# Neighbourhood attention in a two-layer encoder: scores as plain fp32 matmuls on 64x32 pieces with five key blocks per 32 queries, the product with v on 64x64 quarters

## The chip, the cores and the metric

One core of a Trainium2 chip runs the whole program. The metric is the device time of one execution in microseconds, the median over several runs. Engines are named as in the profile: PE is TensorE, DVE VectorE, ACT ScalarE, POOL GpSimd, SP the SyncE queue that issues nearly all DMAs.

## What is computed

Two encoder layers over 512 tokens with 1024 features and 16 heads of 64. Layer A mixes tokens with dilated sliding-window attention in three groups, layer B with attention over a two-dimensional neighbourhood. The change is in layer B alone. Its tokens form a grid of 8 rows and 64 columns; queries are taken in blocks of 16 columns, and each block sees a slab of 32 columns in all 8 rows, masked to the 16 columns round the query, with a learned bias by row and column distance:

```python
def mixer_b(hn, w_in, w_out, q_gain, k_gain, rpb):
    q, k, v, gate = jnp.split(hn @ w_in, 4, axis=-1)
    q = rms_norm(q.reshape(b, s, N_HEADS, HEAD_DIM), q_gain) * (HEAD_DIM ** -0.5)
    k = rms_norm(k.reshape(b, s, N_HEADS, HEAD_DIM), k_gain)
    ...
        logits = jnp.einsum('bhcqd,bhrcjd->bhcqrj', qr, kr) + bias
        logits = jnp.where(col_valid[:, :, None, :], logits, NEG_INF)
        p = jax.nn.softmax(logits.reshape(b, N_HEADS, n_cb, NA_COL_BLOCK, wr * NA_SLAB), axis=-1)
        out = jnp.einsum('bhcqrj,bhrcjd->bhcqd', p, vr)
    ...
    y = y * jax.nn.silu(gate)
    return y @ w_out
```

Every layer is `x + mixer(rms_norm(x))`, all in float32. The kernel returns the final x, transposed by the host's layout.

## The kernel before

**Precision.** The large projections are done in fp32r. A value is split into a high part (a cast) and a low part (value less high), and `mm3` adds three products: high by high, high by low, low by high. ScalarE casts the high part of each weight (`wh`, L133), VectorE or GpSimd subtracts for the low part (`wl`, L139). Activations are split in the same way (`hn_h`, `hn_l`, and `y` in two halves). Layer A's attention uses plain fp32 matmuls on pieces of the array: scores on 64x32, the product with v on 64x64 quarters (`by_quarters`), whose two halves of the keys lie in two PSUM banks. `whole` puts these together: ScalarE copies the one (L803), VectorE adds the other (L804).

**Order.** TensorE's order is written by the program. A generator `main` yields after each piece of projection (`acc`), a generator `side` holds the attention; `run` interleaves them by a simulated clock that each matmul advances. For layer B the table `B_PLAN` says at which clock the scores and the values of each of eight head pairs (0 to 7) come. Values of a pair wait, besides, for its weights to be back from DRAM. `later_on` puts off a DMA or a small job by simulated time, `chores` are the halves of the gate's function (`silu`, L817). The other engines run in order too; a scheduler merges their instructions, and `keep_in_program_order` holds some in the order in which they are written. SP issues in order. PSUM has eight banks: four for `acc`, four (`bank`) for all the rest.

**Layer B's attention** for one head pair:

- the projection leaves q and k, ScalarE evacuates them (`rawq`, L544), GpSimd squares (L312), VectorE sums (L313); the inverse root comes from small steps on VectorE or GpSimd (L113 to L125); VectorE multiplies (L332, four instructions) and transposes (L737, two), and DMAs bring q and k into the layout of the scores (`bd`, then `vv` or `rawq`).
- `side_b` splits q and k into `qkb`: ScalarE L1226, L1227 and L780, VectorE L1228 and L1232, GpSimd L1229 for a copy of q's edge.
- scores: 24 fp32r matmuls on 64x128 pieces, 256 columns each, into four banks `log`.
- softmax: VectorE adds the bias `eb` and takes the minimum (the sign is turned), ScalarE exponentiates (L1276) and scales (L1282); rows are 256 wide, or 128 with two parts.
- the weights are transposed in 32x32 pieces (L905), written to DRAM and read back (`pt`, L918) so that keys lie on partitions.
- values: `side_by_side`, 12 matmuls (24 records) on 128x64 pieces into one bank `o`.
- `put_y`: VectorE multiplies with the gate (L858), ScalarE casts the high part of y (L861), GpSimd subtracts for the low part (L864); for pair 7 VectorE does.

**The out product** (`out_product`) multiplies y with the output weights into eight tiles of 128 features: four in `acc` banks over the first six pairs, then three in `acc2` banks over the same, then pairs 6 and 7 (`late`) for all seven, then the eighth tile in two halves of the tokens. Between pairs' values stand the `acc` matmuls of this product. `residual` loads the x to be added into the memory that held `pt`; it is written to SP's queue after values 6 and after values 7.

Of the kernel before, what the change touches and what calls it, by code (L numbers as in the profile page):

```python
# [22 lines left out]
P = 128  # L23
# [9 lines left out]
LINE = 384 + 2 * 448  # L33

# [12 lines left out]
    ("scores", 7, 176700), ("values", 5, 180000), ("values", 6, 198000), ("values", 7, 213000),  # L47
# [5 lines left out]
def tile_hybrid_encoder(  # L53
# [41 lines left out]
    eb_d = dr.tile([16, P, 384], F32, name="eb_d")  # L95
# [46 lines left out]
    def blocks():  # L142

        for hc in range(NHC):
            b = hc * A_HC
            first = hc == NHC - 1
            yield from ((b + 512 * KT * (i ^ first), 512, KT) for i in range(2))
            if hc == NHC - 1:
                yield b - A_HC + 1152 * KT, 128, KT
            yield b + 1024 * KT, 128, KT  # L150
            if hc != NHC - 2:
                yield b + 1152 * KT, 128, KT
        yield from outs(A_OUT, 1)
# [5 lines left out]
        yield from outs(B_OUT, 2)  # L159

    def outs(b, late):

        k = KT - late
        for n, ks in ((512, k), (384, k)) + ((512, 1), (384, 1)) * late + ((128, KT),):
            yield b, n, ks
            b += n * ks
# [12 lines left out]
    def splits():  # L179
# [22 lines left out]
        while ahead:  # L202
            raw, cols, n = ahead.pop(0)
            step = 384 if n == 384 else 512
            for c in range(0, cols, step):
                queue.append((*split(raw[:, c : c + step], step), min(n, step)))
# [30 lines left out]

    def mm3_heads(os, lh, ll, rh, rl, last):

        for n, (l, r) in enumerate(((lh, rh), (lh, rl), (ll, rh))):  # L240
            for hd in range(2):
                hs = slice(64 * hd, 64 * hd + 64)
                matmul(os[hd], l(hs), r(hs), share=2, start=(n == 0), stop=(last and n == 2))
# [220 lines left out]
    def bias_rows():  # L464
# [10 lines left out]
        def spread_out(rows, cols, first, n, src, o):  # L475
            dst = bass.AP(
                eb_d.tensor, eb_d.offset + rows * 16 * 384 + first * 384 + cols, [[16 * 384, 32], [384, n], [1, src[1]]]
            )
            t, width = src[0], src[0].shape[1]
            tc.keep_in_program_order(  # L480
                nc.sync.dma_start(
                    dst, bass.AP(t.tensor, t.offset + rows * width + o, [[width, 32], [-8, n], [1, src[1]]])
                )
            )

        for n, r in enumerate(range(0, P, 32)):
            later_on(30000 + 40000 * n, partial(spread_out, r, 0, 0, 16, (lb_d, 256), 120))
            later_on(45000 + 40000 * n, partial(spread_out, r, 256, 0, 8, (gb_d, P), 56))
            later_on(55000 + 40000 * n, partial(spread_out, r, 256, 8, 8, (gb_d, P), 120))
# [292 lines left out]
    def side_by_side(o, mms, first=True):  # L782


        for i, (d, v, r) in enumerate(mms):
            for hd in range(2):
                hs = slice(64 * hd, 64 * hd + 64)
                matmul(d(o[hs]), v(hs), r(hd), start=(first and i == 0), stop=(i == len(mms) - 1))

# [95 lines left out]
    def bias_b(hc):  # L885
        e = wk.tile([P, 2, 384], F32, tag="e12", name="eb")
        for hd in range(2):
            m = nc.sync.dma_start(e[:, hd, :], eb_d[2 * hc + hd].rearrange("(r c) x -> c r x", r=8))
            tc.keep_in_program_order(m)
        return e  # L890
# [229 lines left out]
    def out_product(key, sink, late, halves=False):  # L1120
# [5 lines left out]
        def step(k, tiles, hl=None):  # L1126
            h, l = hl or next(wsteps)
            for f in tiles:
                i = f if f < 4 else (f - 4) % 3
# [20 lines left out]
        for f in range(4, 7):  # L1150
            acc[f] = bank("acc2")
        for k in range(KT - late):
            yield from step(k, range(4, 7))
        for k in range(KT - late, KT):
            yield key, k, "y"
            yield from step(k, range(4))
            yield from step(k, range(4, 7))
        acc[7] = ps_acc.tile([P, 512], F32, tag="acc", name="acc")
        if not halves:
            for k in range(KT):  # L1160
                yield from step(k, (7,))
# [49 lines left out]

    def side_b(hc):
        if hc >= 1 and hc + 1 < NHC:
            st["e", hc + 1] = bias_b(hc + 1)
        raw = st.pop(("raw", hc))
        e = st.pop(("e", hc))
        landed, left = raw
        assert not left[0]
        qk = wk.tile([P, 2 * EXT + 2 * S], F32R, tag="q12", name="qkb", bufs=1)
        qh, ql = qk[:, :EXT], qk[:, EXT : 2 * EXT]  # L1220
        kh, kl = (qk[:, 2 * EXT + S * n : 2 * EXT + S * n + S].rearrange("p (t x) -> p t x", t=4) for n in range(2))
        tokens = lambda t: t[:, :S].rearrange("p (i t r) -> p t i r", i=4, t=4)
        src = lambda f: landed[:, :, f, :]
        q_src = src(0).rearrange("p t (i r) -> p t i r", i=4)
        first = lambda t: t[:, S:EXT].rearrange("p (t r) -> p t r", t=2)
# [6 lines left out]
        m = nc.vector.scalar_tensor_tensor(kl, src(1), gk[:, 3:4], kh.bitcast(F32), op0=ALU.mult, op1=ALU.subtract)  # L1232
        tc.keep_in_program_order(m)
        yield 3800
        pt, turners = pq[:, 2048 * (hc % 2) : 2048 * (hc % 2) + 2048], []

        at = lambda a, hd, i: 448 * a + 224 * hd + 32 * i

        def scores(u):
            lgs = lgs_of[u] = [bank("log") for _ in range(2)]  # L1240
            for b in (2 * u, 2 * u + 1):
                i0, step = (b, 1) if b < 3 else (0, 3)
                m = lambda t_, hs: sb(t_[hs], 32 * i0, [[32 * step, 2], [P, 4], [1, 32]])
                qs = slice(64 + P * b, 192 + P * b)
                o = 256 * (b % 2)
                mm3_heads(
                    [lg[:, o : o + 256] for lg in lgs],
                    lambda hs: qh[hs, qs], lambda hs: ql[hs, qs], lambda hs: m(kh, hs), lambda hs: m(kl, hs), True,
                )

        lgs_of = {}

        def softmax(hd, u, lg):
            pr = wk.tile([P, 512], F32, tag="p", name="p", bufs=4)
            mns = wk.tile([P, 8], F32, tag="mnb", name="mns", bufs=4)
            for b in (2 * u, 2 * u + 1):
                mn = mns[:, 4 * (b % 2) : 4 * (b % 2) + 4]
                o = 256 * (b % 2)
                if b < 3:
                    parts = ((slice(0, P), o),)  # L1260
                    n, ec = 256, 0
                else:
                    parts = ((slice(0, 64), o + P), (slice(64, P), o))
                    n, ec = 128, 256
                for rows, c in parts:
                    nc.vector.tensor_tensor_reduce(
                        out=pr[rows, o : o + n],
                        in0=lg[rows, c : c + n],
# [246 lines left out]
```

## Time and profile before

| | |
|---|---|
| median of 3 runs | 806.82 us (806.59 to 807.04) |
| profiled execution | 806.53 us, its span 804.7 us |
| PE busy | 799.6 us (99%) |
| DVE, ACT, POOL busy | 538.9 (67%), 447.8 (56%), 230.1 us (29%) |
| waits of PE that the profile lists | 0.9, 0.6, 0.4, 0.2 us |
| layer B's scores and values in the chain | 8 times about 1.64, 8 times about 1.69 us |

A line of the profile is read so: the chain gives start, duration, engine, the program's name and line, and the number of records. In groups, `64*32 64x128` is the piece of the array and the shape (partitions x columns), then the count, the busy time, the mean of one in ns, and the idle time of the engine just before. In the timeline `x4` groups neighbours, and the bracket gives the idle time before and what ended it. A plain fp32 matmul has two records, an fp32r matmul one.

### The profile page before, as it was taken

The page shows a single profiled execution, that of the slowest core. Times are in us where ns is not written, and L with a number is a line of the kernel's source. Part 1 is how long each engine was busy: PE and PEld are TensorE (multiplying, and loading weights), DVE is VectorE, ACT ScalarE, POOL GpSimd, SP SyncE. Part 2 cuts the span into 40 slices and gives each one's busy share as a digit, 9 for nine tenths or more (in the row PEclk, how much of TensorE's full clock was granted, in tenths as well). Part 3 has the DMA queues.
Part 4 walks back from the last instruction along what each step waited for, and adds up shares of the span by engine and source line. Part 5 has one row for each costly group of instructions (what it writes and reads, how often), then busy time and mean ns, then how long its engine had stood idle before and what let it go on. Part 6 is the DMA issues. An engine that isn't in the chain of part 4 may idle for free.

```text
span 804.7 us, 16419 instructions
## 1 busy us (share of the span) xinstructions
PE 799.6 (99%) x6078; PEld 655.5 (81%) x6078; DVE 538.9 (67%) x1375; ACT 447.8 (56%) x934; POOL 230.1 (29%) x372
## 2 busy tenths in 40 slices
PE   9999999999999999999999999999999999999998
PEld 7888888888888888888888888888888887778787
DVE  7474575676577577477567766638646989997824
ACT  7442745745745744754654675436346675757721
POOL 3242432442441532532432331110312224040100
PEclk9999999999999999999999999999999999999999
DMA  8578587877977976977987955167264797698664
GB/s 291 159 204 255 164 223 236 241 212 204 267 215 221 306 226 208 305 221 209 273 239 217 279 177 168 44 226 241 84 201 124 223 258 204 201 269 238 179 210 158
DMA packets 93585, 172.58 MB, mean 214 GB/s; under 512 B 12160, under 2 KB 51216, under 8 KB 93504
## 3 DMA queue, kind: packets, MB, share of 16 engines
q1 hardware_dynamic: 93360, 171.26, 72.1%
q8 instruction: 48, 0.79, 0.4%
q14 instruction: 33, 0.27, 0.1%
q10 hardware_dynamic: 144, 0.26, 0.1%
HBM read 127.84 MB, written 49.82 MB: 221 GB/s over the span
## 4 chain that ended last, share of the span: by engine, by line
PE 93%; DVE 3%; ACT 3%; DMA 1%; POOL 0%; issue 0%; SPq 0%; DVEq 0%
PE acc L227 83%; PE log L227 5%; PE o L227 4%; ACT p L1276 1%; PE tp L231 1%; DVE wl L139 1%; ACT p L1282 1%; DMA wraw<-in_w 1%; DVE rawq L332 0%; ACT rawq L544 0%; ACT wh L133 0%; DVE rawq L737 0%; PE pa L227 0%; POOL sq L312 0%; ACT x L426 0%
## 5 line engine op out<-in xcount | busy, mean ns | idle before, releaser
L227 PE MATMUL acc<-wh,hn_h 128*128 128x512 f32 x704 | 277.3, 395 | 0.4 <-ACT rawq L544 0.4
L227 PE MATMUL acc<-wl,hn_h 128*128 128x512 f32 x704 | 273.7, 390 | 0.6 <-POOL wl L139 0.6
L227 PE MATMUL acc<-wh,hn_l 128*128 128x512 f32 x704 | 273.6, 389 | 0.0
L133 ACT CAST wh<-wraw 128x512 fp32r<-128x512 f32 (+1 forms) x259 | 157.7, 612 | 207.1 <-PE acc L227 180.0
L139 DVE TENSOR_TENSOR wl<-wraw,wh 128x512 fp32r<-128x512 f32 (+1 forms) x188 | 137.5, 734 | 145.5 <-ACT wh L133 145.0
L139 POOL TENSOR_TENSOR wl<-wraw,wh 128x512 fp32r<-128x512 f32 (+1 forms) x72 | 96.7, 1342 | 231.2 <-ACT wh L133 197.0
L227 PEld LDWEIGHTS acc<-wh,hn_h 128*128 128x128 f32 x704 | 132.1, 188 | 31.8 <-issue 3.3
L227 PEld LDWEIGHTS acc<-wh,hn_l 128*128 128x128 f32 x704 | 132.1, 188 | 27.9
L227 PEld LDWEIGHTS acc<-wl,hn_h 128*128 128x128 f32 x704 | 132.2, 188 | 27.7 <-POOL wl L139 1.4
L312 POOL TENSOR_TENSOR sq<-rawq 128x256 f32<-128x256 f32 (+1 forms) x82 | 59.9, 741 | 108.4 <-ACT rawq L544 95.5
L227 PE MATMUL acc<-y,wh 128*128 128x512 f32 (+1 forms) x272 | 81.5, 383 | 0.0
L997 ACT ACTIVATE p<-p,mn 128x512 f32<-128x512 f32 (+1 forms) x64 | 44.8, 701 | 60.3 <-DVE mn L986 60.3
L227 PE MATMUL acc<-hn_h,wh 128*128 128x512 f32 x192 | 75.7, 394 | 0.0
L227 PE MATMUL acc<-hn_l,wh 128*128 128x512 f32 x192 | 74.8, 389 | 0.0
L227 PE MATMUL acc<-hn_h,wl 128*128 128x512 f32 x192 | 74.7, 389 | 0.0
L905 DVE STREAM_TRANSPOSE tr<-p 128x512 f32<-128x512 f32 (+1 forms) x88 | 59.0, 681 | 20.8 <-ACT p L824 11.4
L313 DVE TENSOR_REDUCE ss<-sq 128x4 f32<-128x256 f32 (+1 forms) x96 | 47.6, 506 | 31.9 <-POOL sq L312 31.4
L227 PEld LDWEIGHTS acc<-y,wh 128*128 128x128 f32 x272 | 48.8, 188 | 9.4 <-issue 0.9
L227 PE MATMUL acc<-y,wl 128*128 128x512 f32 (+1 forms) x136 | 51.3, 377 | 0.0
L332 DVE TENSOR_TENSOR rawq<-rawq,rs 128x256 f32<-128x256 f32 (+1 forms) x96 | 48.2, 563 | 2.3 <-POOL rs L125 1.9
L544 ACT ACTIVATE rawq<-acc,rs_n 128x512 f32<-128x512 f32 (+1 forms) x76 | 45.8, 613 | 0.3
L824 ACT ACTIVATE p<-p,mn 128x512 f32<-128x512 f32 (+1 forms) x64 | 44.3, 700 | 2.1 <-DVE mn L823 2.0
(144 smaller groups left out, 918.7 us busy)
## 6 DMA issues: line engine op xcount, KB each, us to landing
wraw<-in_w SPq DMA_DIRECT2D x119, 512.0 KB, 5.6
td<-tr SPq DMA_DIRECT2D x14, 1024.0 KB, 8.1
pt<-td SPq DMA_DIRECT2D x56, 256.0 KB, 4.6
qd<-rawq SPq DMA_DIRECT2D x7, 1536.0 KB, 7.2
qt<-qd SPq DMA_DIRECT2D x28, 384.0 KB, 6.6
td<-tr SPq DMA_DIRECT2D x8, 896.0 KB, 5.4
pt<-td SPq DMA_DIRECT2D x32, 224.0 KB, 6.7
bd<-rawq SPq DMA_DIRECT2D x8, 512.0 KB, 3.2
```

The lines of the kernel that those rows point to most:

```text
L133: nc.scalar.copy(h, raw)
L139: eng.tensor_sub(l, raw, h.bitcast(F32))
L227: nc.tensor.matmul(o, l, r, **kw)
L231: nc.tensor.transpose(o, i, ident)
L312: nc.gpsimd.tensor_mul(to, v, v)
L313: nc.vector.tensor_reduce(ss[:, i * ns : (i + 1) * ns], sq.rearrange("p (a b) -> p a b", b=64), axis=AX.X, op=ALU.add)
L332: m = nc.vector.tensor_mul(v, v, by)
L544: nc.scalar.activation(dst, src, AF.Copy, scale=rs_n[:, i : i + 1])
L824: nc.scalar.activation(pr, pr, AF.Copy, scale=mn[:, 3:4])
L905: nc.vector.transpose(dst, src[:, :n].rearrange(order, b=4, k=32, **({"g": 2} if apart else {})))
L997: nc.scalar.activation(row, row, AF.Exp, bias=mn[:, 1:2], scale=-1.0, accum_out=mn[:, 2:3])
L1276: nc.scalar.activation(pr[:, o : o + n], pr[:, o : o + n], AF.Exp, bias=mn[:, 0:1], scale=-1.0, accum_out=mn[:, 2:3])
```

## The change

Layer B's q and k are no longer split. The scores take q as it landed and one tile `kx` in which ScalarE puts k, scaled; GpSimd copies 64 columns at each end, so that any five neighbouring blocks of 32 keys are contiguous. For each of 16 blocks of 32 queries and both heads there is one fp32 matmul of 160 columns on a 64x32 piece. Softmax rows are all 160 wide, and the bias in DRAM is laid out for that (14 writes instead of 12, eight loads per pair instead of two, into a tile kept for two pairs). Twelve small transposes take the place of four. The weights go through DRAM in half key tiles, each with 192 queries (six blocks, `RUN`).

The values use `by_quarters` and `whole` from layer A: 32 fp32 matmuls into two banks, ScalarE's copy and VectorE's add after them. As two banks are now used, the out product of layer B holds two tiles in `acc2` (`more` = 2) rather than three; the seventh tile is its own pass over the eight pairs, after the late ones. The weights are laid out in that order. In `B_PLAN` the values of pair 7 are due at 207000 instead of 213000.

```diff
-    ("scores", 7, 176700), ("values", 5, 180000), ("values", 6, 198000), ("values", 7, 213000),
+    ("scores", 7, 176700), ("values", 5, 180000), ("values", 6, 198000), ("values", 7, 207000),
...
     def side_b(hc):
-        tc.keep_in_program_order(nc.scalar.copy(tokens(qh), q_src))
-        tc.keep_in_program_order(nc.scalar.copy(first(qh), landed[:, 0:2, 0, 0:32]))
-        tc.keep_in_program_order(nc.vector.tensor_sub(tokens(ql), q_src, tokens(qh.bitcast(F32))))
-        nc.gpsimd.tensor_copy(ql[:, S:EXT], ql.bitcast(F32)[:, 0:64])
-        yield 700
-        tc.keep_in_program_order(scaled(kh, src(1), 3))
-        m = nc.vector.scalar_tensor_tensor(kl, src(1), gk[:, 3:4], kh.bitcast(F32), op0=ALU.mult, op1=ALU.subtract)
-        tc.keep_in_program_order(m)
-        yield 3800
+        kx = wk.tile([P, 20 * 32], F32, tag="e12", name="kx")
+        mid = kx[:, 64 : 64 + S].rearrange("p (i t r) -> p t i r", i=4, t=4)
+        tc.keep_in_program_order(scaled(mid, landed[:, :, 1, :].rearrange("p t (i r) -> p t i r", i=4), 3))
+        nc.gpsimd.tensor_copy(sb(kx, 0, [[576, 2], [1, 64]]), sb(kx, 128, [[320, 2], [1, 64]]))
+        yield 3500
...
         def scores(u):
+            lgs = [bank("log") for _ in range(2)]
+            for t in (2 * u, 2 * u + 1):
+                o = W5 * (t % 2)
+                for j in range(4):
+                    k = 32 * (4 * j + t)
+                    for hd in range(2):
+                        hs = slice(64 * hd, 64 * hd + 64)
+                        matmul(lgs[hd][32 * j : 32 * j + 32, o : o + W5], landed[hs, t, 0, 32 * j : 32 * j + 32],
+                               kx[hs, k : k + W5], share=2, start=(t % 2 == 0), stop=(t % 2 == 1))
...
         def weigh():
-            o = bank("o")
-            side_by_side(o, mms)
-            return o
+            os = [bank("o") for _ in range(2)]
+            jobs = [(n, m, RUN * m + 128 * n, 4, P * m) for m in range(4) for n in range(2)]
+            for m in range(3):
+                jobs += [(0, m + 1, RUN * m + 256, 2, P * m + 64), (1, m, RUN * m + RUN, 2, P * m + P)]
+            jobs += [(0, 3, 3 * RUN + 320, 1, 480), (1, 0, 0, 1, 0)]
...
+            by_quarters(os, mms)
+            return whole(os)
...
-    def out_product(key, sink, late, halves=False):
+    def out_product(key, sink, late, more):
-        for f in range(4, 7):
+        for f in range(4, 4 + more):
             acc[f] = bank("acc2")
...
+        for f in range(4 + more, KT):
+            acc[f] = ps_acc.tile([P, 512], F32, tag="acc", name="acc")
+            if f == 7 and more < 3:
+                break
             for k in range(KT):
-                yield from step(k, (7,))
+                yield from step(k, (f,))
```

The order of the instructions moves with it. In the changed kernel lines have other numbers: L332 is L329, L737 is L733, L804 is L792, L817 is L805, L858 is L846, L861 is L849, L864 is L852, L139 is L142, L227 is L231, L1208 is L1206, L780 is L776.

The first place is round the scores of pair 3. VectorE in the kernel before, from the low parts of q and k (`qkb`) to the transposes of the next head norm; `gt` is the gate of pair 1, which is multiplied with `o`, `na` and `rs` are steps of the head norm's inverse root, `rawq` is what it scales:

```order
L1228 TENSOR_TENSOR qkb<-vv,qkb 128x4x4x32
L120 SCALAR_TENSOR_TENSOR na<-na,nv 128x16
L1232 SCALAR_TENSOR_TENSOR qkb<-vv,gk,qkb 128x512
L858 TENSOR_TENSOR gt<-gt,o 128x512
L1208 TENSOR_TENSOR gx<-acc,rs_half 128x512
L121 SCALAR_TENSOR_TENSOR rs<-na,rs 128x16
L332 TENSOR_TENSOR rawq<-rawq,rs 128x2x4x32 x4
L139 TENSOR_TENSOR wl<-wraw,wh 128x512
L737 STREAM_TRANSPOSE rawq<-rawq 128x2x256 x2
```

VectorE at the same place after the change:

```order
L123 SCALAR_TENSOR_TENSOR na<-na,nv 128x16
L1206 TENSOR_TENSOR gx<-acc,rs_half 128x512
L124 SCALAR_TENSOR_TENSOR rs<-na,rs 128x16
L142 TENSOR_TENSOR wl<-wraw,wh 128x512
L121 TENSOR_TENSOR na<-rs 128x16
L123 SCALAR_TENSOR_TENSOR na<-na,nv 128x16
L124 SCALAR_TENSOR_TENSOR rs<-na,rs 128x16
L329 TENSOR_TENSOR rawq<-rawq,rs 128x2x4x32 x4
L733 STREAM_TRANSPOSE rawq<-rawq 128x2x256 x2
L792 TENSOR_TENSOR ow<-ow,o 128x512
L846 TENSOR_TENSOR gt<-gt,ow 128x512
```

The multiplication of pair 1 stood ahead of the head norm's products; now it stands, with the add of the two halves (`ow`), behind products and transposes. GpSimd, same place, before: the copy of q's edge (`qkb`) for pair 3, the last steps of an inverse root, then the low part of pair 1's y.

```order
L1229 CAST qkb<-qkb 128x64
L113 TENSOR_SCALAR nv<-ss 128x16
L114 TENSOR_SCALAR rs<-nv 128x16
L118 TENSOR_TENSOR na<-rs 128x16
L123 TENSOR_TENSOR na<-na,nv 128x16
L124 TENSOR_SCALAR na<-na 128x16
L125 TENSOR_TENSOR rs<-rs,na 128x16
L118 TENSOR_TENSOR na<-rs 128x16
L864 TENSOR_TENSOR y<-gt,y 128x512
```

And after:

```order
L126 TENSOR_TENSOR na<-na,nv 128x16
L127 TENSOR_SCALAR na<-na 128x16
L128 TENSOR_TENSOR rs<-rs,na 128x16
L852 TENSOR_TENSOR y<-gt,y 128x512
L1247 COPY kx<-kx 128x2x64
```

The copy for pair 3 stood ahead of the low part of y and now stands behind it. On ScalarE the key's copy for pair 3 (L776) likewise follows the cast of pair 1's y (L849).

The second place is the end of the out product. TensorE before, round the values of pair 7 (`o`); the first four `acc` rows and the three `acc2` tiles (`acc_8927` to `acc_8929`) still belong to pair 6, and the last row reads the y of pair 7:

```order
L227 MATMUL o<-pt,rawk 64x128 x2
L227 MATMUL acc<-y,wh 128x512 x2
L227 MATMUL acc<-y,wl 128x512
L227 MATMUL acc<-y,wh 128x512 x2
L227 MATMUL acc<-y,wl 128x512
L227 MATMUL acc_8927<-y,wh 128x512 x2
L227 MATMUL acc_8927<-y,wl 128x512
L227 MATMUL acc_8928<-y,wh 128x512 x2
L227 MATMUL acc_8928<-y,wl 128x512
L227 MATMUL acc_8929<-y,wh 128x512 x2
L227 MATMUL acc_8929<-y,wl 128x512
L227 MATMUL acc<-y,wh 128x512 x2
```

TensorE there after the change; `acc_9211` and `acc_9212` are the two `acc2` tiles for pair 6, and the last row reads the y of pair 7:

```order
L231 MATMUL o<-pt,rawk 64x128 x16
L231 MATMUL o<-pt,rawk 64x64 x12
L231 MATMUL o<-pt,rawk 64x32 x4
L231 MATMUL acc_9211<-y,wh 128x512 x2
L231 MATMUL acc_9211<-y,wl 128x512
L231 MATMUL acc_9212<-y,wh 128x512 x2
L231 MATMUL acc_9212<-y,wl 128x512
L231 MATMUL acc<-y,wh 128x512 x2
```

Fifteen matmuls stood between values 7 and its first reader, six do now. VectorE there after the change, with the two halves of the gate's function (L805) between the add and the multiplication:

```order
L792 TENSOR_TENSOR ow<-ow,o 128x512
L805 SCALAR_TENSOR_TENSOR gt<-eg,gt 128x256 x2
L846 TENSOR_TENSOR gt<-gt,ow 128x512
L142 TENSOR_TENSOR wl<-wraw,wh 128x512
L852 TENSOR_TENSOR y<-gt,y 128x512
```

Before, L817 and L858 followed each other with no add ahead of them, and nothing stood between L858 and L864.

More of the change, by code (lines that the diff above doesn't have):

```diff
@@ L158, in blocks, with outs @@
             b += n * KT
[L159 to L164, printed above, removed]
+        yield from outs(B_OUT, 2, 2)
+    def outs(b, late, more):
+        k, m = KT - late, P * more
+        for n, ks in ((512, k), (m, k)) + ((512, 1), (m, 1)) * late + ((128, KT),) * (4 - more):
             yield b, n, ks
@@ L1308, in side_b @@
+            by_quarters(os, mms)
+            return whole(os)
+        lgs_of = [scores(u) for u in range(2)]
         held = []
-        for u in range(2):
-            scores(u)
         for u in range(2):
```

222 lines of the change are left out of this document (106 added, 116 removed).

## Prediction

> **What bounds the kernel now.** I read the page first, then the waits, the chain, and the timeline round the places that the change touches.
>
> ```profile
> span 804.7 us, 16419 instructions
> PE 799.6 (99%) x6078; PEld 655.5 (81%) x6078; DVE 538.9 (67%) x1375; ACT 447.8 (56%) x934; POOL 230.1 (29%) x372
> PE 93%; DVE 3%; ACT 3%; DMA 1%; POOL 0%; issue 0%; SPq 0%; DVEq 0%
> ```
>
> TensorE is the bound: 99% busy and 93% of the chain. The waits say how little it stands still.
>
> ```profile
> PE busy L398 <- DVE warm L387: 0.9, 1, 0.9
> PE acc L227 <- POOL wl L139: 0.6, 1, 0.6
> PE acc L227 <- ACT rawq L544: 0.4, 1, 0.4
> PE log L227 <- DVE qkb L1232: 0.2, 1, 0.2
> ```
>
> So a shorter attention block is won in full, and a new wait of TensorE is lost in full, unless an engine that feeds it comes late. The profiled execution took 806.53 us, 1.83 more than its span; the median of the three runs is 806.82. I sum against 806.53 and add 0.29. A measurement can tell about 0.2% from no change: faster is under 805.2, slower over 808.4.
>
> **The blocks on TensorE.** The chain has scores and values of layer B (24 instructions) and, already in the form to which they go, layer A's (96 and 120). An fp32 matmul shows as two records, an fp32r one as one.
>
> ```profile
> 510.15 1.84 PE log L227 x96
> 523.35 2.72 PE o L227 x120
> 608.41 1.64 PE log L227 x24
> 610.05 22.64 PE acc L227 x99
> 769.63 1.69 PE o L227 x24
> L227 PE MATMUL log<-qt,q 64*32 64x128 f32 x896 | 19.5, 271 | 0.0
> L227 PE MATMUL log<-k,q 64*32 64x256 f32 x224 | 9.5, 382 | 0.0
> L227 PE MATMUL o<-pt,v0x 64*64 64x128 f32 x256 | 10.3, 270 | 0.0
> L227 PE MATMUL o<-pt,v0x 64*64 64x64 f32 x192 | 7.1, 217 | 0.0
> ```
>
> The 64x32 pieces grow from 271 to 382 ns over 128 columns, 0.87 ns a column. Eight run side by side. Layer A's block is 64 records of 128 columns, 16 of 192 and 16 of 256, 160 on average, so 96 x 160/8 = 1920 columns deep: 1.67 us and a remainder of 0.17. The new scores are 64 records of 160 (4 query tiles x 4 blocks x 2 heads x 2 records), 1280 deep: 1.11 + 0.17 = 1.28; by records alone, 1.84 x 64/96 = 1.23. I take 1.30 against 1.64: 0.34 less, bounds 0.24 and 0.41.
>
> The 64x64 quarters grow by 53 ns over 64 columns, 0.83 ns a column, four side by side. Layer A's 2.72 us hold 64 records of 128 columns and 56 of 64, 11776/4 = 2944 deep, so 2.44 + 0.28. The new values have per head 8 jobs of 128 columns, 6 of 64 and 2 of 32, 1472 in all; two heads and two records over four quarters leave 1472 deep: 1.22 + 0.28 = 1.50; by records 2.72 x 64/120 = 1.45. I take 1.48 against 1.69: 0.21 less, bounds 0.14 and 0.33. Eight of each: -4.4 us (bounds -3.0 and -5.9).
>
> One rule speaks against this. The Trainium skill, "TensorEngine Tiling (Array Packing)", section Instruction Overhead, gives each matmul about 60 cycles whatever its columns, and warns against tiling a dimension that is already small. As an estimate at that page's 60 cycles and the 2.4 GHz of "TensorE: Matmul & The Clock Gate", 64 records would take 1.6 us, the blocks would save under 1 us in all, and the sum would be near 811. Layer A's row disagrees, 96 records in 1.84 us being 19 ns each, and the row decides.
>
> **The splits go.** Scores 4 waited in its middle for the key's low part:
>
> ```profile
> 693.48 0.39 PE L227 MATMUL log<-qkb 64*128 64x256 f32 x2
> 694.04 1.59 PE L227 MATMUL log<-qkb 64*128 64x256 f32 x22 [0.18 <-DVE qkb L1232]
> ```
>
> The third matmul starts 0.56 after the first; at 1.59/22 = 0.07 each it would have been 0.14. The wait goes: -0.4 us (bounds -0.2, the wait as the profile books it, and -0.4). The splits' other instructions on VectorE, ScalarE and GpSimd lie beside TensorE's work and count nothing. The 0.4 for ScalarE's `rawq` I leave standing; at most it goes too.
>
> **A new wait at scores 3.** Here the order moves. The product of head pair 1 now ends in a copy and an add (`ow`), and VectorE has that add and the following multiplication behind four products and two transposes of the key's head norm. ScalarE's key copy for pair 3 stands behind the cast of y, and GpSimd's copy of the key's edge behind its subtraction. TensorE's scores 3 wait for both copies. All that follows on TensorE waits with them. Before, the multiplication stood ahead of the products:
>
> ```profile
> 669.11 0.41 DVE L313 TENSOR_REDUCE ss<-sq 128x4 f32<-128x256 f32 x1
> 669.44 0.17 DVE L120 SCALAR_TENSOR_TENSOR na<-na,nv 128x16 f32<-128x16 f32 x1
> 669.73 0.69 DVE L139 TENSOR_TENSOR wl<-wraw,wh 128x512 fp32r<-128x512 f32 x1
> 671.88 0.69 DVE L858 TENSOR_TENSOR gt<-gt,o 128x512 f32<-128x512 f32 x1
> 672.49 0.68 DVE L1208 TENSOR_TENSOR gx<-acc,rs_half 128x512 f32<-128x512 f32 x1
> 672.60 0.62 ACT L861 CAST y<-gt 128x512 fp32r<-128x512 f32 x1 [2.03 <-DVE gt L858]
> 673.29 2.58 DVE L332 TENSOR_TENSOR rawq<-rawq,rs 128x256 f32<-128x256 f32 x4
> 674.11 1.47 POOL L864 TENSOR_TENSOR y<-gt,y 128x512 fp32r<-128x512 f32 x1
> 676.41 1.29 DVE L737 STREAM_TRANSPOSE rawq<-rawq 128x512 f32<-128x512 f32 x2
> 676.82 1.70 PE L227 MATMUL log<-qkb 64*128 64x256 f32 x24
> 642.49 1.39 DVE L332 TENSOR_TENSOR rawq<-rawq,rs 128x256 f32<-128x256 f32 x4
> L804 DVE TENSOR_TENSOR ow<-ow,o 128x512 f32<-128x512 f32 x8 | 5.5, 687 | 11.5 <-ACT ow L803 11.5
> L471 POOL COPY lb<-rp 128x128 f32<-128x128 f32 x1 | 0.3, 291 | 0.1
> ```
>
> On this clock the last reduction ends at 669.52. Five small steps at 0.17, one `gx` at 0.68 and one `wl` at 0.69 bring VectorE to 671.74. The four products take 1.39 where GpSimd is idle and 2.58 where it subtracts y; now that subtraction comes later and only GpSimd's small norm steps run, so I take 2.0, nearer the first: 673.74. Transposes 1.29, add 0.69, multiplication 0.69: 676.41. Cast 0.62, subtraction 1.47: 678.5. The edge copy (128x128 in a row of 0.29): 678.8. ScalarE's key copy, of the cast's size and right behind it, is done by then. TensorE comes at 676.82 less three `acc` matmuls that now follow the scores (22.64/99 = 0.23 each) less 0.21 of the shorter values: 675.93. A wait of 2.9 us. With 1.39 and y in 1.30 (another row of it, below) it is 2.1; with 2.58 it is 3.4.
>
> On the 2.0 the Trainium skill, "SBUF — State Buffer", section Who interferes with whom, says that a VectorE instruction with two SBUF inputs contends with a GpSimd one that reads SBUF. By it the products would go at 1.39 wherever GpSimd rests, and the wait would be 2.3; the two rows agree, but GpSimd doesn't rest here throughout.
>
> **A new wait at y of pair 7.** Between values 7 and the first matmul that reads its y there were 15 `acc` matmuls; now 6.
>
> ```profile
> 785.29 0.75 DVE L817 SCALAR_TENSOR_TENSOR gt<-eg,gt 128x256 f32<-128x256 f32 x2
> 787.55 0.69 DVE L858 TENSOR_TENSOR gt<-gt,o 128x512 f32<-128x512 f32 x1 [1.50 <-PE o L227]
> 788.92 0.69 DVE L864 TENSOR_TENSOR y<-gt,y 128x512 fp32r<-128x512 f32 x1 [0.69 <-ACT y L861]
> L803 ACT COPY ow<-o 128x512 f32<-128x512 f32 x8 | 4.7, 587 | 24.9 <-PE o L227 24.9
> ```
>
> Before, y was there 2.06 us after values 7 ended (787.55 to 789.61), under 15 x 0.23 = 3.4 us of cover. Now: copy 0.59, add 0.69, the two gate steps (0.75, which ran before the block ended and now stand behind the add), multiplication 0.69, cast 0.62, subtraction 0.69: 4.03, and some 0.1 for a `wl` between. The cover is 6 x 0.23 = 1.4, and the first of the reading matmuls needs only the cast: 1.6. 4.1 to 4.2 less 1.6: +2.6 us (2.2 to 3.0), with nothing behind it to take it up.
>
> **The rest of the tail.** Values 7 comes 48 `acc` matmuls (10.9 us) after values 6, instead of 63 (14.5). Its input is read behind the residual's loads:
>
> ```profile
> 771.36 1.56 SPq L1175 DMA_DIRECT2D pt<-xm_d  x2
> 773.13 1.30 POOL L864 TENSOR_TENSOR y<-gt,y 128x512 fp32r<-128x512 f32 x1 [9.16 <-ACT y L861]
> 773.44 1.85 SPq L918 DMA_DIRECT2D pt<-td  x4
> DMA to landing us min/median/max: 5.5/6.1/6.8
> ```
>
> The fourth read issues at about 774.9 and lands by 781.7 at most, 10.4 after values 6 ended at 771.3. It just fits; I take +0.3 with the y of pair 5 (0 to 1.3). Eight bias loads for two on SyncE's queue, each about 0.4 to issue: some 2.5 us more delay per pair, against reads that, in the pair just shown, lie 4 us ahead of their block. Nothing.
>
> Sum: -4.4 - 0.4 + 2.9 + 2.6 + 0.3 = +1.0. On 806.53 that is 807.5, on the median 807.8.
>
> **Rivals.** (a) One of the two waits is absent: the order says who stands behind whom, and VectorE could come to pair 1's add sooner than row times say. For it: VectorE loses two splits per pair. Against: its norm chain starts from sums that GpSimd and TensorE release. Without scores 3's wait, 804.9; without y's, 805.2; without both, 802.3. Chance 0.17, mostly faster.
>
> (b) Pair 7's reads come late. The place is values 7, the point a landing of over 10.9 us after values 6, half a microsecond past the row above; every microsecond over is paid. For it: residual loads of the same queue land together with them. Against: the row, 6.8 at most. At a landing of 8.3 instead of 6.8 it costs 1.0 beside my 0.3, at 9.3 it costs 2.0: 808.8 to 809.8. Chance 0.20, mostly slower.
>
> (c) The wait at scores 3 lets TensorE's rate fall. After its first idle stretch TensorE ran ten matmuls at 0.45 each, twice the 0.23 later:
>
> ```profile
> 0.92 4.46 PE L398 MATMUL busy<-ones 128*128 128x512 f32 x10 [0.92 <-DVE warm L387]
> ```
>
> If that came back for as long, 4.46 us at half rate lose 2.2: 810.0. It decides from a wait that no row has, since the longest is 0.9. "TensorE: Matmul & The Clock Gate", Trainium skill, in its section on M=128, puts it at a whole window of about 3.4 us idle; my 2.9 stays below, my upper bound reaches it. Chance 0.07, slower.
>
> **The numbers.** My own case has 0.56: 0.38 within 0.2%, 0.15 slower, 0.03 faster; by the bounds of its terms, not all at once, 805.9 to 809.6. With (a) faster 0.14 and same 0.03, (b) same 0.05 and slower 0.15, (c) slower 0.07: faster 0.17, same 0.46, slower 0.37. The range takes in one absent wait below and (b) and (c) above.
>
> **What would show it.** Right: score blocks near 1.30 and value blocks near 1.48 in the chain; among TensorE's waits one of about 3 us before scores 3, put down to GpSimd's `kx`, and one of about 2.6 after values 7, put down to `y`. Wrong: blocks no shorter than 1.64 and 1.69, either wait below 1 us, or a wait over 1 us at another place.

## The result and the profile after

The changed kernel takes 812.54 us in the median (810.42 to 816.14, seven runs), the kernel before 806.82 (806.58 to 807.27, seven runs): a ratio of 1.0071, interval 1.0052 to 1.0090. The forecast was 807.8, and its dearest rival, (c), 810.0; the direction was left open, and the measured time lies beyond both. The spread is new: the kernel before stays within 0.7 us, the changed one within 5.7. Part of it shows in the mean granted clock of TensorE, where 1.000 is full speed: 1.000 in the run of 810.42, 0.998 in 811.09 and 812.93, 0.996 in the other four, which still lie 4.3 us apart. The profiled execution is the slowest of the seven, 816.14, with a span of 814.3, so its waits are not those of a usual one. One execution of e7 (891.66 us) and one of e10 (2054.52 us) below stand far outside of the others, and the times given leave them out.

First the page of the changed kernel, then TensorE's waits in it.

```profile
span 814.3 us, 17799 instructions
...
PE 799.7 (98%) x6718; PEld 655.7 (81%) x6718; DVE 527.0 (65%) x1398; ACT 441.3 (54%) x925; POOL 228.8 (28%) x373
```

```profile
PE log L231 <- POOL kx L1247: 5.0, 2, 2.6
PE acc L231 <- ACT y L849: 1.8, 1, 1.8
PE o L231 <- DMA pt<-tdb: 1.5, 1, 1.5
PE acc L231 <- ACT rawk L540: 1.5, 1, 1.5
```

Five places, where one or two were forecast: `kx` twice (scores 3 and scores 7), the y of pair 7, the weights of pair 7, and an evacuation. Set side by side by the count of `acc` matmuls, the two executions differ as follows. A wait is counted here from start to start, which makes it up to 0.5 us longer than the idle time in the list of waits:

| place | us against before |
|---|---|
| eight scores, eight values on TensorE | -4.3 |
| old stalls at scores 4 and ahead of the evacuation near 703 | -1.0 |
| scores 3: wait 2.5, then slow matmuls | +4.1 |
| evacuation near 730 | +1.7 |
| scores 7: wait 2.7, then slow matmuls | +4.1 |
| values 7 (wait 1.6) and y of pair 7 (2.5) | +4.3 |
| before layer B | +0.5 |
| sum (measured at the last matmul: +9.5) | +9.4 |

**Scores 3**, the timeline of the changed kernel, VectorE, ScalarE, GpSimd and TensorE:

```profile
668.47 0.41 DVE L310 TENSOR_REDUCE ss<-sq 128x4 f32<-128x256 f32 x1
...
670.79 1.47 DVE L329 TENSOR_TENSOR rawq<-rawq,rs 128x256 f32<-128x256 f32 x4
672.30 1.30 DVE L733 STREAM_TRANSPOSE rawq<-rawq 128x512 f32<-128x512 f32 x2
...
673.53 0.65 DVE L792 TENSOR_TENSOR ow<-ow,o 128x512 f32<-128x512 f32 x1
...
674.21 0.75 DVE L846 TENSOR_TENSOR gt<-gt,ow 128x512 f32<-128x512 f32 x1
675.00 0.62 ACT L849 CAST y<-gt 128x512 fp32r<-128x512 f32 x1 [1.92 <-DVE gt L846]
675.52 0.72 ACT L776 ACTIVATE kx<-vv,gk 128x512 f32<-128x512 f32 x1
675.69 1.27 POOL L852 TENSOR_TENSOR y<-gt,y 128x512 fp32r<-128x512 f32 x1
676.90 0.76 POOL L1247 COPY kx<-kx 128x128 f32<-128x128 f32 x1
```

The chain runs link by link as forecast: products, transposes, add, multiplication, cast, subtraction, copy, then TensorE. The products took 1.47, nearer to 1.39 than the 2.0 that I took, and VectorE came to them 0.95 earlier than reckoned; against that the edge copy took 0.76 instead of 0.29, and TensorE itself was there 0.6 earlier. TensorE's idle time was 2.4 us, against 2.9. The order was right; that the size came so near is in part luck, since these errors cancel.

What follows it wasn't in the sum. The windows round the place (behind the window's length stand PE, PEld, DVE, ACT and POOL with busy time and count, then the granted clock, the DMA share and GB/s):

```profile
676.00:680.00 4.00, 2.29 (x66) 1.78 (x67) 1.81 (x10) 1.72 (x7) 1.66 (x2) 0.86 1.07 256
680.00:684.00 4.00, 4.00 (x15) 3.16 (x14) 3.34 (x19) 4.00 (x18) 0.00 (x0) 0.72 0.71 226
```

The clock falls behind the wait, and TensorE does 15 matmuls in four microseconds. Windows of four microseconds blur the fall. Cut where the granted clock changes, they show it whole, first at scores 3, then at scores 7:

```profile
675.43:678.84 3.41, 1.13 (x64) 1.10 (x64) 1.05 (x3) 1.31 (x3) 2.18 (x3) 1.00 1.05 247
678.84:682.26 3.42, 3.42 (x26) 2.46 (x8) 3.15 (x22) 3.24 (x15) 0.00 (x0) 0.50 1.02 315
...
757.35:760.76 3.41, 3.20 (x66) 2.61 (x67) 2.54 (x9) 1.66 (x4) 1.43 (x2) 0.50 0.90 316
```

The clock is halved for 3.41 us and then whole again, so that one fall costs at most 1.7 us. The mean clock of a profiled execution counts its falls: 1.000 or 0.999 where there is none, 0.998 with one, 0.996 with two (or, in e7, with one of twice the length). By that, the median execution of the changed kernel, at 0.996, has two.

**The evacuation near 730**, ScalarE, where the keys of the next pairs stand behind the cast of pair 3's y:

```profile
731.17 0.62 ACT L849 CAST y<-gx 128x512 fp32r<-128x512 f32 x1 [2.26 <-DVE gx L846]
731.70 2.42 ACT L540 ACTIVATE rawk<-acc,rs_n 128x512 f32<-128x512 f32 x4
```

In the kernel before the order was the same, but that cast started at 727.46 and the keys at 728.50, and TensorE didn't wait.

**Scores 7**, in the chain of the changed kernel:

```profile
735.74 1.18 SPq L881
...
736.97 1.31 SPq L881
...
740.59 9.48 DMA eb<-eb_d
750.07 0.02 issue
750.08 6.25 DMA vv<-bd
...
757.21 0.30 POOL kx L1247
...
757.56 2.49 PE log L231 x64
```

and SyncE's queue at that place, in the timeline:

```profile
735.74 8.17 SPq L881 DMA_DIRECT2D eb<-eb_d  x8
...
744.76 0.33 SPq L1230 DMA_DIRECT2D pt<-tdb  x1
745.63 4.76 SPq L744 DMA_DIRECT2D vv<-bd  x4
```

The eight bias loads hold the queue for 8.2 us, 1.0 each, and the reads of pair 7's q and k (`vv`) wait behind them. In the kernel before, at the same place:

```profile
731.67 2.13 SPq L888 DMA_DIRECT2D eb<-eb_d  x2
...
736.33 1.74 SPq L748 DMA_DIRECT2D vv<-bd  x4
```

So two bias loads held the queue for 1.07 each already there, and the four reads took 1.74 to issue where they now take 4.76. The bursts of pairs 2 to 7 in the changed kernel hold it for 5.2 to 9.4 us. In the profiles that keep these bursts, pair 7's held it for 6.1 to 8.4 us, and scores 7 waited 2.6 us (the changed kernel), 2.4 (e10) and 1.9 (e4), but not at all in e3, with 6.8.

**The tail**, timeline:

```profile
777.42 0.80 SPq L1173 DMA_DIRECT2D pt<-xm_d  x2
...
780.78 0.44 SPq L1230 DMA_DIRECT2D pt<-tdb  x1
...
790.01 1.65 PE L231 MATMUL o<-pt,rawk 64*64 64x128 f32 x64 [1.51 <-DMA pt<-tdb]
...
792.26 0.69 DVE L792 TENSOR_TENSOR ow<-ow,o 128x512 f32<-128x512 f32 x1 [1.96 <-ACT ow L791]
792.87 0.76 DVE L805 SCALAR_TENSOR_TENSOR gt<-eg,gt 128x256 f32<-128x256 f32 x2
793.66 0.69 DVE L846 TENSOR_TENSOR gt<-gt,ow 128x512 f32<-128x512 f32 x1
794.38 0.62 ACT L849 CAST y<-gt 128x512 fp32r<-128x512 f32 x1 [0.72 <-DVE gt L846]
795.03 0.69 DVE L852 TENSOR_TENSOR y<-gt,y 128x512 fp32r<-128x512 f32 x1
```

Here too the chain is the one forecast, 4.08 us from the end of values 7 to the last step. Values 7 starts 9.2 us after the last read of its weights was issued, where before such a read had landed after 6.8 at most.

### The profile page after: what moved, and what is told of

Read it like the earlier page. It is cut to its first block, busy times and chain, and to the rows that moved or that the text cites. A ratio compares the mean times of both kernels' runs of the same rounds, so it can differ in the third digit from the quotient of the medians.

```text
span 814.3 us, 17799 instructions
## 1 busy us (share of the span) xinstructions
PE 799.7 (98%) x6718; PEld 655.7 (81%) x6718; DVE 527.0 (65%) x1398; ACT 441.3 (54%) x925; POOL 228.8 (28%) x373
## 5 line engine op out<-in xcount | busy, mean ns | idle before, releaser
L231 PE MATMUL acc<-wh,hn_h 128*128 128x512 f32 x704 | 278.2, 396 | 0.4 <-ACT hn_h L419 0.4
L231 PE MATMUL acc<-wl,hn_h 128*128 128x512 f32 x704 | 274.3, 390 | 0.2 <-POOL wl L142 0.2
L231 PE MATMUL acc<-wh,hn_l 128*128 128x512 f32 x704 | 274.2, 390 | 0.0
L142 DVE TENSOR_TENSOR wl<-wraw,wh 128x512 fp32r<-128x512 f32 (+2 forms) x187 | 136.9, 733 | 159.6 <-ACT wh L136 159.0
L142 POOL TENSOR_TENSOR wl<-wraw,wh 128x512 fp32r<-128x512 f32 (+1 forms) x72 | 96.5, 1340 | 227.0 <-ACT wh L136 177.6
L231 PEld LDWEIGHTS acc<-wh,hn_h 128*128 128x128 f32 x704 | 132.6, 189 | 32.6 <-issue 4.2
L231 PEld LDWEIGHTS acc<-wh,hn_l 128*128 128x128 f32 x704 | 132.4, 188 | 27.9
L231 PEld LDWEIGHTS acc<-wl,hn_h 128*128 128x128 f32 x704 | 132.7, 188 | 27.4 <-POOL wl L142 0.9
L231 PE MATMUL acc<-y,wh 128*128 128x512 f32 (+1 forms) x272 | 82.3, 386 | 2.0 <-ACT y L849 1.8
L231 PE MATMUL acc<-hn_h,wh 128*128 128x512 f32 x192 | 75.8, 395 | 1.5 <-ACT rawk L540 1.5
L231 PE MATMUL acc<-hn_h,wl 128*128 128x512 f32 x192 | 74.8, 390 | 0.0
L231 PE MATMUL acc<-hn_l,wh 128*128 128x512 f32 x192 | 74.8, 389 | 0.0
L231 PEld LDWEIGHTS acc<-y,wh 128*128 128x128 f32 x272 | 49.0, 189 | 12.2 <-ACT y L849 2.2
L231 PE MATMUL acc<-y,wl 128*128 128x512 f32 (+1 forms) x136 | 51.4, 378 | 0.0
L329 DVE TENSOR_TENSOR rawq<-rawq,rs 128x256 f32<-128x256 f32 (+1 forms) x96 | 48.2, 563 | 2.3 <-POOL rs L128 1.9
L900 DVE STREAM_TRANSPOSE tr<-p 128x512 f32<-128x512 f32 x56 | 39.0, 706 | 11.4 <-ACT p L812 11.4
```

The lines of the kernel that those rows point to most:

```text
L142: eng.tensor_sub(l, raw, h.bitcast(F32))
L231: nc.tensor.matmul(o, l, r, **kw)
L329: m = nc.vector.tensor_mul(v, v, by)
L900: nc.vector.transpose(dst, src[:, :n].rearrange(order, b=4, k=32, **({"g": 2} if apart else {})))
```

## The experiments

The theory after the result: each loss has a place of its own in the order. Scores 3 and the evacuation suffer from a pair's y ahead of more urgent work, scores 7 from the burst of bias loads on SyncE's queue, the tail from the residual's place and six matmuls of cover, and the rate of TensorE falls behind some waits. The rival: a general cause, the traffic or the small fp32 pieces, so that a wait removed here comes back there. Base is 812.54; ratios are to the kernel before on the same chip.

**Filling the wait (e1_fill).**

```diff
+            for _ in range(11 * fill):      # scores 3 and 7 only
+                nc.tensor.matmul(lgs[0], wide(P), wide(S), start=True, stop=True)
```

> The changed kernel with eleven extra matmuls (128x512, at 0.23 us each about 2.5 us) ahead of the scores of pairs 3 and 7, into a bank that the scores then overwrite; they fill the time in which TensorE waits for kx. Theory (the idle stretch itself makes TensorE's rate fall): the granted clock stays at 1.00 behind both places, the acc matmuls behind scores 3 come at 0.23 and not 0.43 us, and the time falls by 2 to 3 us against the changed kernel's 812.5, to about 810, with less spread between runs. Rival (the small fp32 pieces or the switch to them lower the rate, or the chip does it by itself): the clock falls as before and the time stays at 812 to 813.

815.75 us, 1.0113 (1.0093 to 1.0132), with no less spread (812.21 to 817.93). The time missed; the mechanism didn't. The windows of this kernel:

```profile
676.00:680.00 4.00, 3.99 (x76) 3.02 (x75) 2.02 (x11) 1.72 (x8) 1.45 (x2) 1.00 1.05 249
680.00:684.00 4.00, 3.77 (x29) 2.88 (x31) 3.34 (x20) 4.00 (x18) 0.00 (x0) 1.00 0.64 214
```

With TensorE busy, the clock stays at 1.00 here and round scores 7, the same scores follow, and the place of scores 3 costs 1.0 us less. At scores 7 the fill takes its 2.6 us also in executions that would have waited less, and the waits of the tail grew (2.5 for `y` where it was 1.8, 1.9 for weights where it was 1.5), with a fall of the clock behind the one for `y`; I take that to be where the median went, though only one execution was profiled. So the idle time lowers the rate, not the pieces.

**Without the bias loads (e2_no_bias).**

```diff
-        if hc >= 1 and hc + 1 < NHC:
-            bias_b(hc + 1)
```

> The changed kernel without the bias loads of pairs 2 to 7, which use the bias of pairs 0 and 1: 48 of 64 loads on SyncE's queue are left out. Theory (the bursts of eight loads hold up the queue, and with it the key of pair 7): the wait before scores 7 (2.6 us, with slow matmuls 3.8) goes, the waits at scores 3 (2.5) and at the y of pair 7 (2.6) stay; about 808 to 809. Rival (the loads are hidden and pair 7's key is late for another reason, its own write and read): the wait before scores 7 stays above 2 us and the time at 812.

812.43 us, 1.0066 (1.0054 to 1.0079); the profiled execution 809.86. There scores 7 has no wait at all, and all other waits stay. The median is a miss: it is 0.1 below the changed kernel's where some 4 were expected. That profile's clock is 1.000, that of the three slowest runs 0.996, so the rest of the median is put down to the rate behind the remaining waits, which no profile of those runs shows. In a usual execution, then, the bias loads cost the changed kernel little; the wait of 2.6 at scores 7 is shown for its slowest one alone.

**Values 1 earlier (e3_early).**

```diff
-    ("values", 1, 108000), ("scores", 3, 108700), ...
+    ("values", 1, 103000), ("scores", 3, 108700), ...
```

> The changed kernel with the values of pair 1 due at 103000 instead of 108000, some 24 acc matmuls earlier, so that pair 1's product is through before the head norm of the next pairs, and the key copies of pair 3 stand ahead of pair 1's y on ScalarE and GpSimd. Theory (scores 3 waits because of that order): its wait of 2.5 us and the slow stretch behind it (1.6) go, the others stay: about 808 to 809. Rival (kx of pair 3 is late because its data are): the wait stays over 1.5 us, time at 812.

814.59 us, 1.0099 (1.0085 to 1.0113): 2.0 more than the changed kernel, with intervals that overlap a little. Scores 3 has no wait any more, but values 1 and 2 wait for weights (2.2 and 1.8), which TensorE's waits total, with 0.8 before values 7, as

```profile
PE o L231 <- DMA pt<-tdb: 4.8, 3, 2.2
```

That looked like the rival, waits that come back elsewhere. **Both together (e6_early_no_bias)** tells:

```diff
-    ("values", 1, 108000), ...
+    ("values", 1, 103000), ...
...
-            bias_b(hc + 1)
```

> Values of pair 1 at 103000 as before, and the bias loads of pairs 2 to 7 left out (these pairs use the bias of pairs 0 and 1). With the loads in place that edit took scores 3's wait away and gave two new ones before values 1 and 2 (2.3 and 1.8 us), for weights not back from memory. Theory (those weights are late by the bursts on the queue): both waits go, scores 3 has none, about 809 (812.4 of the kernel without these loads, less 2.5 of wait and up to 1 of slow matmuls). Rival (the weights can't be back by then even on a free queue): a wait above 1 us stays before values 1, and the time at 811 to 812.

809.21 us, 1.0031 (1.0021 to 1.0041). Neither wait is there. The weights were late by the bias loads; the two edits need each other.

**The tail (e4_tail).**

```diff
+            if hc == NHC - 2:
+                yield "wait", ("back", NHC - 1), 0      # residual behind the reads of pair 7
             if hc >= NHC - 2:
                 yield from residual(xm_d, 4 * (hc % 2))
...
+            if hc == NHC - 1:
+                for _ in st["gate", hc][1]:             # gate steps ahead of values 7
+                    pass
             put_y(hc, weigh(), False, hc == NHC - 1)
```

> The changed kernel with the residual's first loads issued behind the reads of pair 7's weights instead of ahead of them, and pair 7's two gate steps ahead of values 7 on VectorE instead of behind its add. Theory: the wait before values 7 (1.7 us in the profile) goes and the wait for the y of pair 7 falls from 2.6 by 0.75 to about 1.9; together 2.4 less, about 810. Rival (pair 7's reads are late by the memory's load and not by their place in the queue): the first wait stays, and only 0.7 is won.

810.30 us, 1.0045 (1.0031 to 1.0058), 2.2 less. The wait for weights is gone, and the one for `y` stands at 1.2 where it was 1.8: as the theory has it.

**Loads spread (e5_spread), and on another queue (e7_pool_queue).**

```diff
-                load(j, hd)
+                later_on(1200 * (2 * j + hd), partial(load, j, hd))
...
-            tc.keep_in_program_order(nc.sync.dma_start(...eb...))
+            tc.keep_in_program_order(nc.gpsimd.dma_start(...eb...))
```

> The changed kernel with the eight bias loads of a pair issued 1200 apart on the simulated clock instead of in one burst. Theory (a burst of eight holds SyncE's queue for 8 to 9 us, and the reads of weights and keys behind it come late): no wait before scores 7 in any profile, the wait before values 7 (1.9 us) gone or halved, scores 3 and the y of pair 7 as before; about 810.5. Rival (it is the number of loads, not the burst): the queue is as late as before, 812 to 813.

> The changed kernel with its bias loads on GpSimd's queue instead of SyncE's: the same bytes and descriptors, another issuer. Theory (place in SyncE's queue): waits before scores 7 and values 7 gone, 2 us less, about 810.5, unless GpSimd's issue delays kx. Rival (the traffic itself in the DMA engines): weights and keys as late as before, 812 to 813.

(The spreading is for pairs 2 to 7.) Spread: 811.42 us, 1.0062 (1.0049 to 1.0075), which by its interval is not clear of the changed kernel. Scores 7 has no wait; values 7 keeps 1.4, so that one is not the burst's. On GpSimd's queue: 817.21 us, 1.0140 (1.0122 to 1.0159). Scores 7 has no wait there either, and the four reads of pair 7's q and k take 1.89 to issue, but on GpSimd eight loads (676.50 to 681.13) stand ahead of its copy for pair 3, and one wait was

```profile
PE log L231 <- POOL kx L1247: 6.6, 1, 6.6
```

The place in the queue matters, not the bytes, as far as scores 7 goes (in e7 TensorE also came there 4.7 us later); in this order GpSimd is no better place.

**All together, first try (e8_combined)**, with values 3 put ahead of scores 5 to clear the evacuation:

```diff
-    ("scores", 5, 145000), ("values", 3, 145000), ...
+    ("values", 3, 143000), ("scores", 5, 145000), ...
```

> Spread bias loads, values of pair 1 at 103000, values of pair 3 at 143000 ahead of scores 5 (so that its y is cast before ScalarE evacuates the keys and not in front of it), residual behind the reads of pair 7's weights, pair 7's gate steps early. Theory (each named wait has its own cause and place): waits at scores 3 (2.5), ahead of the evacuation near 730 (1.6), before scores 7 and values 7 go, y of pair 7 keeps 1.9; blocks save 4.6 and the old stall 0.4: about 804 to 805, under the kernel before. Rival (the waits move on to the next place, as with values 1): 808 or more, with new waits for weights before values 1, 2 or 3.

809.66 us, 1.0036 (1.0024 to 1.0049), a miss of the same kind as the change's own: the waits at scores 3, the evacuation, scores 7 and values 7 are gone, and scores 5 has the pattern of scores 3, a pair's y ahead of `kx`:

```profile
PE log L231 <- POOL kx L1250: 3.8, 1, 3.8
PE acc L231 <- ACT y L849: 1.2, 1, 1.2
```

**Second try (e9_all), and its burst (e10_all_burst).** Values 3 goes behind the evacuation instead, values 7 comes twelve matmuls earlier. Besides, the margin that values 7 leave to the return of their weights falls from 3500 to 1000 on the simulated clock, and the residual's first two loads are set 600 apart:

```diff
-    ("values", 3, 143000), ("scores", 5, 145000), ..., ("values", 7, 207000),
+    ("scores", 5, 145000), ("values", 3, 160500), ..., ("values", 7, 204500),
```

> Everything so far that took a wait away, and values 3 put behind the evacuation of the keys instead of ahead of scores 5: spread bias loads, values 1 at 103000, values 3 at 160500 (30 acc matmuls later), pair 7's gate steps early, the residual's first loads behind the reads of pair 7's weights, and values 7 twelve acc matmuls earlier, so that 18 (4.1 us) lie between them and the reader of their y. Theory (each wait has its own place in the order, and none is needed): no wait over 0.6 us in layer B, blocks save 4.6 us and the old stalls near 0.8, the clock stays at 1.00: 801.5 to 803. Rival (the waits move on, as scores 5 showed with 4.2 us): above 805, with a new wait at the next scores or values.

```diff
-                    later_on(1200 * (2 * j + hd), partial(load, j, hd))      # e10 against e9
+                    load(j, hd)
```

> The same kernel with the eight bias loads of a pair again in one burst. Theory (the burst holds SyncE's queue): waits for weights before values 1 and 2 (2.3 and 1.8 us before, when values 1 came early) and perhaps for the key of pair 7; 3 to 6 us longer than the kernel with spread loads. Rival (spreading does nothing once the order is right): within 0.5 us of it.

801.45 us (801.17 to 801.64), 0.9938 (0.9925 to 0.9951): faster than both kernels, and the spread is gone as well. All that is left of TensorE's waits:

```profile
PE busy L395 <- DVE warm L384: 0.9, 1, 0.9
```

and two blocks of its chain:

```profile
606.96 1.27 PE log L231 x64
...
639.88 1.47 PE o L231 x64
```

With the loads in one burst again: 810.06 us, 1.0042 (1.0027 to 1.0058), 8.6 more, where 3 to 6 were expected. In its profile scores 7 waits 2.4, and values 1 and 2 wait 4.2 together; SyncE's queue ahead of values 2, and the clock behind the wait:

```profile
662.11 8.40 SPq L881 DMA_DIRECT2D eb<-eb_d  x8
670.61 0.39 SPq L195 DMA_DIRECT2D wraw<-in_w  x1
671.29 3.82 SPq L1230 DMA_DIRECT2D pt<-tdb  x4
```

```profile
683.40 2.81 PE L231 MATMUL o<-pt,rawk 64*64 64x128 f32 x64 [1.82 <-DMA pt<-tdb]
```

```profile
684.00:688.00 4.00, 4.00 (x62) 3.61 (x55) 1.67 (x6) 0.74 (x2) 0.00 (x0) 0.59 0.49 152
```

**One part undone (e11_undo_values1, e12_undo_tail).** The edits of e3 and of the whole tail, each taken back from the best kernel.

```diff
-    ("values", 1, 103000), ...
+    ("values", 1, 108000), ...
```

> The best kernel so far (801.45) with one part undone: values 1 again at 108000, so that the key copies of pair 3 stand behind pair 1's y. Prediction's term: a wait of 2.9 us before scores 3, 804.3. With the price of the fall in rate behind it, as in the changed kernel's profile, 1 to 2 us more in those executions where it falls: 804 to 806, wider between runs. Rival (the wait at scores 3 needs the late queue too): under 1 us of wait, 802.

```diff
-    ..., ("values", 7, 204500),
+    ..., ("values", 7, 207000),
...
-            if hc == NHC - 2:
-                yield "wait", ("back", NHC - 1), 0
...
-                for _ in st["gate", hc][1]:
-                    pass
```

> The best kernel so far with the tail undone: residual's loads again ahead of the reads of pair 7's weights, gate steps of pair 7 late, values 7 at 207000. Prediction's terms: 2.6 us for the y of pair 7 and 0 to 1.3 for the weights, 804.4. As measured in the changed kernel's profile: 2.6 and 1.7, 805.7. Rival (pair 7's reads were late by the burst of bias loads, which is spread here): the weights' wait is gone, 804.0.

Values 1 back: 805.33 us, 0.9990 (0.9981 to 0.9999), 3.9 more. The profile has the wait at scores 3 (2.4) and a clock of 1.00 there, 804.55. The six runs with a clock of 0.999 or 1.000 take 803.91 to 805.33, the five with 0.997 or 0.998 take 805.70 to 807.19; the medians of the two groups are 1.8 apart. Tail back: 807.86 us, 1.0016 (1.0008 to 1.0025), 6.4 more. Both of its waits are in the profile, 2.5 and 0.2 for `y`, 1.2 for the weights, and 0.9 for the y of pair 5, which the sum had within its 0.3; the loads were spread, so the burst isn't their cause.

## Why the prediction was wrong

- **The blocks** were right: 1.27 and 1.47 where 1.30 and 1.48 stood, -4.3 in all against -4.4. The rule of a fixed price per matmul (the Trainium skill, "TensorEngine Tiling (Array Packing)", Instruction Overhead), by which 64 records would have taken 1.6 if each counts as a matmul, does not hold for these overlapping pieces: 1.27 for 64 is 20 ns each. That the time by this rule, near 811, lies close to the measured one is luck, for the loss is elsewhere. The stall at scores 4 went, as said, and so did the one of ScalarE's `rawq` that the sum left standing; together -1.0 for -0.4.
- **The wait at scores 3** was right in mechanism and near in size, 2.4 to 2.5 for 2.9; undone alone in e11 it costs 3.9 with what follows it.
- **The wait for pair 7's y** was right, 2.5 for 2.6.
- **The step that failed** is the rest of the sum: behind the two waits it has +0.3 for all other places, "Nothing" for the bias loads, and a rate of TensorE that never falls. For a usual execution the profiles show three things in its place. The evacuation near 730, scores 3's pattern, which I followed at one pair only, costs 1.7; it is in all eight profiles that have values 3 at 145000 with an idle time of 1.4 to 1.8, and it is gone where values 3 move (e8, e9). The weights of pair 7 come late, by 0.8 to 1.9 where the residual stands ahead of them. And the rate falls twice, by the median's clock, at up to 1.7 each. As an estimate from these figures that is some 6.5 us against 0.3; less 1 for the places that came out smaller than forecast, it comes near the 4.7 by which the forecast was low.
- **"Eight bias loads for two on SyncE's queue ... Nothing"** was wrong as well, in price and in cover, but weighs less in the usual execution. I priced a load at 0.4, where a row of the kernel before had 1.07, and looked for cover at the last pair, the one pair in whose time no bias is loaded; the loads before were larger (192 KB against 80), yet in the changed kernel too one takes 0.6 at the least. In the profiled execution the loads give scores 7 its wait, 2.7 with some 1.5 of slow matmuls; e2, e5 and e7 all take it away. Yet the median falls by only 0.1 without the loads (e2) and by 1.1 with them spread (e5). They cost 8.6 us in the order of e9, where values 1 come early (e10 against e9).
- **Rival (b) came true** in the profile: values 7 started 9.2 us after the last read, 1.5 of it a wait, against 0.3. The place in the queue decides (e4, e12), the burst does not (e5).
- **Rival (c) came true** at 0.07, and with it up to 1.7 us behind scores 3 and again at scores 7 in the profiled execution. I let it hang on a wait above 3.4 us. "TensorE: Matmul & The Clock Gate" (the Trainium skill, section "What's actually happening") says besides that the window of about 3.4 us is free-running. The traces agree with that: each of the ten falls ahead of the last matmuls, in fourteen profiles, lasts 3.41 us (6.83 once, in e7), and where a profile has two they start a whole number of such stretches apart, 23 in the changed kernel (78.51 us) and 32 in e3 (109.23). They differ on the condition, for falls came behind idle times of 1.8 to 6.6 us, and waits of 2.4 and 2.5 went free. What tells most of them apart is how a wait lies on these stretches, counted in each profile from where the clock first rises. In e11 the 2.4 us at scores 3 are split between two of them, and the clock stays:

```profile
672.56:675.97 3.41, 2.29 (x11) 1.56 (x9) 2.51 (x4) 1.48 (x4) 2.86 (x8) 1.00 0.63 202
675.97:679.39 3.42, 2.14 (x67) 1.77 (x68) 1.79 (x9) 1.15 (x5) 1.23 (x2) 1.00 0.69 220
```

Counted so in every profile, a fall follows each full-rate stretch in which TensorE was busy for 1.2 us or less (eight such), none in which it was busy for 1.7 or more; between 1.4 and 1.65 it came twice and stayed away three times, which the traces don't explain.

The sum held two waits and 0.3 for the rest; five came in the profiled execution. What stays open is how the 812.54 of a usual execution is shared exactly, since only the slowest was profiled.

## What to carry to other kernels

When TensorE is 99% busy, a cheaper block is won only if the engines and the queue that feed it keep their order: go through every pair, not one, and look for each place where work with time to spare now stands ahead of work that TensorE waits for. Count a queue's hold by what one of its transfers takes in a crowd, here 0.7 to 1.2 us and not 0.4, and look at what stands behind the burst. A wait of about 2 us can cost up to 1.7 more, in one execution and not in the next; and edits that each fail alone (e3) can be the cure together (e6, e9).

## What the runs showed of the hardware

- The granted clock of TensorE was halved for 3.41 us (once for 6.83) behind some idle times of 1.8 to 6.6 us, in some executions and not in others; filling the idle time with matmuls kept it at 1.00 (e1).
- Eight DMAs of 80 KB held SyncE's queue for 5.2 to 9.4 us in the changed kernel, and a single one for 0.6 where e9 spread them (three together still took 3.1):

```profile
657.51 0.62 SPq L881 DMA_DIRECT2D eb<-eb_d  x1
```

- A plain fp32 matmul on 64x32 pieces with 160 columns costs 20 ns a record when eight pieces run side by side, one on 64x64 quarters 23 ns: 1.27 us for a pair's scores and 1.47 for its values.
